# A three-block transformer layer on one core: layer-norm rows rebuilt from the transposed result, small reloads on the load queue, and one raw weight tile more in two rings

## The chip, the core and the metric

The kernel runs on one core of a Trainium2 chip. A core has five engines that work at the same time: TensorE (matmuls, called PE in the profile; PEld are its weight loads), VectorE (DVE), ScalarE (ACT), GpSimd (POOL) and SyncE (SP), which here only issues DMAs. Each engine takes its instructions in order, and semaphores hold an instruction until what it needs is there. Data live in device memory, in the on-chip memory SBUF (128 partitions) and in PSUM, where matmuls write: eight banks of 128 x 512 float32. POOL cannot read PSUM.

The metric is the device time in microseconds (us) of one execution. The kernel before took 5420.15 us, the median of three runs from 5416.47 to 5428.44 us.

## The reference

One layer over 512 tokens of width 2048, in float32. Three sub-layers follow one another, each added to its input and normalised:

```python
h = hybrid_mixer(x, ...)             # mLSTM heads + 16 forgetting-attention heads, gated, merged
x = layer_norm(DN_ALPHA * x + h, ln_w[0], ln_b[0])
h = memory_cross_attention(x, mem, w_xq, w_xkv, w_xo)     # 256 memory rows
x = layer_norm(DN_ALPHA * x + h, ln_w[1], ln_b[1])
h = peer_ffn(x, peer_wq, peer_sub_keys, peer_u, peer_v)   # 16 of 16384 experts per head and token
x = layer_norm(DN_ALPHA * x + h, ln_w[2], ln_b[2])
```

`layer_norm` takes mean and variance over the 2048 features of a token, and scales and shifts each feature: `(x - mu) * rsqrt(var + eps) * w + b`.

## The kernel before

**Tokens and stages.** The 512 tokens are four blocks of 128. Block 0 (`A` in the code) is computed first through the whole mixer, since the others need its state; blocks 1 to 3 (`B`, 384 tokens) follow. On the time axis of the profile: the first stage (to 870 us) is block 0's mixer, and between its groups `memory` projects the 256 memory rows; then (to 1620) `tail_a` takes block 0 through its output projection, both norms, the cross attention and the choice of its experts, alternating with the mLSTM heads of B; then B's `branch_ml` and `fox` (to 2550), `merge`, `residual`, `norm`, `cross`, `residual`, `norm` (to 3290), and B's `query` and top-k. From 3421 the experts: 288 tokens are computed densely over all 16384 experts (`stage_a`, `stage_h`, `stage_o`), and the experts of block 0 and of the last 96 tokens are gathered row by row by indirect DMAs on POOL with multiply-adds on DVE (`gathered`), a side job that `load_w` and `fill` advance a step at a time.

**A weight tile's way.** Every matmul operand is split into a high part (fp32r) and the remainder, and a product is three matmuls. A weight tile of 128 x 1024 comes by a DMA on SP's queue into a tile `raw`; ACT casts it to `whi` (L120); DVE (L123) or, for every `SHARE`-th tile, POOL (L122) subtracts to `wlo`. `raw` is free for the next load once `wlo` is written, so the number of raw tiles (4 in ring `w1` of the first stage, 5 in `w2`, 3 in `w3`, 2 in the ring `V` of the experts' second matrix) says how many loads are under way. `group_ws` holds the weights stationary and uses four large PSUM banks, `group_as` one bank for each token block. There are five large banks (tag `mm`) and three for small work (`sm_bank`).

**A norm.** `residual` leaves rows `r[t][g]` (128 tokens x 512 features; `t` the block, `g` the quarter) and their statistics. `norm` (L595) centres and scales the rows, turns each 128 x 128 piece with a TensorE transpose into a small bank, applies the weight and bias there, where they are one number for each partition, and splits the result into the operand pair of the next product (`X1`, `X2`). Then, for the rows that the next residual adds, it loads weight and bias broadcast over the partitions (L620, L621), multiplies and adds them on POOL (L624, L625; one block on DVE in B's second norm) and stores the rows to scratch memory (L626, `x1d` or `x2d`).

**Order.** The program is written as generators, and a scheduler orders each engine's instructions before the run, so that neighbours in the program can change places within what data and tiles allow; on the chip the order is fixed. Pools reuse memory of earlier pools: a new tile waits for the last use of what lay there. When B's second norm is done, the rows, the attention's tiles and operands are given up, and the tiles of the top-k and of ring `V` take their place.

**Other lines named below.** L956 and L995 reload the mLSTM output `htd` and the attention output `ytd` of B from scratch memory, by DMAs on POOL's queue, into three tiles `hr` and six tiles `t`. L454 is the sigmoid that empties the banks of a gate group of `branch_ml`, L737 the copy of a query group, L751 block 0's expert numbers, L797 and L784 the row updates of the gathered experts, L1028 the load of the 16 sub-key matrices, on ACT's queue. L318 and L327 empty the memory projections' banks into a tile `mo` that POOL's queue stores.

Of the kernel before, what the change touches and what calls it, by code (L numbers as in the profile page):

```python
# [10 lines left out]
F32 = mybir.dt.float32  # L11
# [5 lines left out]
ALU = mybir.AluOpType  # L17
# [14 lines left out]
NDENSE = 288  # L32
GATHERED = ((64, 64), (32, 32))
GB = 48
SHARE = 4
NEG = -1.0e30
ALPHA = 2.0 ** 0.25
EPS = 1e-5
# [8 lines left out]
def build(tc, I, out):  # L47
    nc = tc.nc
    with ExitStack() as ctx:
# [5 lines left out]
        def weights(stack, name, raw, hi, lo):  # L55

            W.update(pool=stack.enter_context(tc.tile_pool(name=name, bufs=1, reuse_waits="tile")), raw=raw, hi=hi, lo=lo)

        xs, x0 = ctx.enter_context(ExitStack()), ctx.enter_context(ExitStack())
        xbp = xs.enter_context(tc.tile_pool(name="x_b", bufs=1))  # L60
        weights(x0, "w1", 4, 3, 2)
        xap = x0.enter_context(tc.tile_pool(name="x_a", bufs=1))

        cnt, turn = [0], [0]
# [240 lines left out]
        def memory(mp):  # L305

            MT = []
            for kt in range(8):
                raw = load_raw(I["memT"][kt], 512)
                a, b = pair(mp, "mt", [P, 512], 16)  # L310
                split(a, b, raw)
                for kk in range(2):
                    MT.append((a[:, kk * MEM:(kk + 1) * MEM], b[:, kk * MEM:(kk + 1) * MEM]))
            for g in range(4):
                def ev_mk(s, b, g=g, k=[]):
                    if s % 2 == 0:
                        k.append(mp.tile([P, 512], F32, tag="mo", bufs=2, name=nm("mo")))
                    nc.scalar.copy(k[-1][:, (s % 2) * MEM:(s % 2 + 1) * MEM], b[:, :MEM])  # L318
                    if s % 2:
                        nc.gpsimd.dma_start(kmd[g, s // 2], k[-1])  # L320

                group_ws(I["w_xkv"][g], MT, MEM, ev_mk)
                yield
            for g in range(4):
                def ev_mv(t, b, g=g):
                    v = mp.tile([P, 512], F32, tag="mo", bufs=2, name=nm("mo"))
                    nc.vector.tensor_copy(v, b)  # L327
                    nc.gpsimd.dma_start(vmd[g, t], v)

                group_as(I["w_xkv"][4 + g], MT, 2, ev_mv)  # L330
                yield
# [260 lines left out]
            nc.vector.scalar_tensor_tensor(sts[:, :, 27], sts[:, :, 24], -1.0, sts[:, :, 26],  # L592
                                           op0=ALU.mult, op1=ALU.mult)

        def norm(R, r, sts, i, dst, cpair, tmp, o, vec=()):  # L595

            for c in range(NK):
                if c % 4 == 0:
                    for t in range(R.nb):
                        y = r[t][c // 4]  # L600
                        if (t + c // 4) % 2:
                            nc.scalar.activation(y, y, AF.Identity, scale=sts[:, t, 26:27], bias=sts[:, t, 27:28])
                        else:
                            nc.vector.tensor_scalar(y, y, sts[:, t, 24:25], sts[:, t, 26:27],
                                                    op0=ALU.subtract, op1=ALU.mult)
                bank = sm_bank()
                for t in range(R.nb):
                    nc.tensor.transpose(bank[:, t * P:(t + 1) * P], r[t][c // 4][:, (c % 4) * P:(c % 4 + 1) * P], ident)
                o.append(cpair())
                w, bb = lnwT[:, i, c:c + 1], lnbT[:, i, c:c + 1]  # L610
                f = tmp(R.n)
                if c % 2:
                    nc.scalar.activation(f, bank[:, :R.n], AF.Identity, scale=w, bias=bb)
                else:
                    nc.vector.tensor_scalar(f, bank[:, :R.n], w, bb, op0=ALU.mult, op1=ALU.add)
                split(*o[-1], f)
            work["hold"] = False
            for g in range(4):
                w, bb = tmp(512), tmp(512)
                nc.gpsimd.dma_start(w, I["ln_w"][i, g * 512:(g + 1) * 512].partition_broadcast(P))  # L620
                nc.gpsimd.dma_start(bb, I["ln_b"][i, g * 512:(g + 1) * 512].partition_broadcast(P))  # L621
                for t in range(R.nb):
                    e = nc.vector if t in vec else nc.gpsimd
                    e.tensor_mul(r[t][g], r[t][g], w)  # L624
                    e.tensor_add(r[t][g], r[t][g], bb)  # L625
                    nc.gpsimd.dma_start(dst[R.b0 + t, :, g], r[t][g])  # L626


        def cross(R, pool, X1, qt, kvt, pt, opair, O):
# [232 lines left out]
        work["share"] = SHARE  # L862
        with tc.tile_pool(name="sa", bufs=1, side="right", reuse_waits="tile") as sa:
            def aq(n=P):
                return sa.tile([P, P], F32, tag="q", bufs=12, name=nm("aq"))

            def at(n=512):
                if n == P:
# [113 lines left out]
        with tc.tile_pool(name="xb", bufs=1, reuse_waits="tile") as xp:  # L982
# [25 lines left out]
            norm(B, r, sts[1], 1, x2d, cpair, tmp, X2, vec=(1,))  # L1008
        x3.close()
        while work["jobs"] is not None:  # L1010
            if next(work["jobs"], None) is None:
# [12 lines left out]
               for t in range(1, TB)}  # L1024

        with tc.tile_pool(name="topk", bufs=1, reuse_waits="tile") as tp:
            keysT = tp.tile([P, 16, P], F32, tag="keysT", name="keysT")
            nc.scalar.dma_start(keysT, I["keysT"])  # L1028
            scs, QB = {}, []
            for g, _ in enumerate(query(B, X2, lambda: tp.tile([P, B.n], F32, tag="qT", bufs=6, name=nm("qT")), QB)):  # L1030
                for t in range(TB - 1, 0, -1):
                    bank = sm_bank()
                    for j in range(4):
                        nc.tensor.matmul(bank[:, j * P:(j + 1) * P], QB[g][j][:, (t - 1) * P:t * P],
                                         keysT[:, 4 * g + j, :], start=True, stop=True)
                    first = t == TB - 1
                    scs[t, g] = tp.tile([P, 512], F32, tag=f"sc{first}", bufs=2 if first else 8, name=nm("sc"))
                    nc.scalar.copy(scs[t, g], bank)
# [244 lines left out]
```

## Time and profile before

| | |
|---|---|
| median of three runs | 5420.15 us (5416.47 to 5428.44) |
| profiled execution | 5381.62 us, span 5379.9 us |
| mean granted TensorE clock | 0.965 |
| busy: PE, DVE, ACT, POOL | 4856.5, 3778.6, 2109.8, 1691.1 us |
| DMA | 1429 MB, mean 266 GB/s |

All durations come from the one profiled execution, whose own time is 38.5 us below the median of the three runs. A matmul's end in the profile is modelled, and matmuls overlap: the step from one start to the next tells more than the duration. A row of a group of instructions reads: line, engine, operation, output <- inputs, shapes, count | busy time, mean of one in ns | idle time of the engine just before them, and what ended it. A row of waits reads: who waited <- for whom: total us, times, longest us; SPq is the load queue of SP.

### The profile page before, as it was taken

To read this page: it belongs to the slowest core of one execution; us is meant where nothing else is said; L and a number is where in the kernel's file an instruction comes from. 1 tells how busy PE (TensorE), PEld (TensorE's weight loads), DVE (VectorE), ACT (ScalarE), POOL (GpSimd) and SP (SyncE) were. 2 spreads that over 40 slices of the span, in tenths; PEclk is the share of its full clock that TensorE was granted. 3 is DMA by queue.
4 is the path that set the end of the run, shared out by engine and by line. 5 is a ranking of instruction groups with operands and counts; after the bars stand their busy time and mean duration, and the time that the engine had idled before them with its cause. 6 is when DMAs were issued, how large, how long until landed. Compare 5 with 4: busy or idle time off the path is not lost. (4 is left out here: it accounts for less than half of the span.)

```text
span 5379.9 us, 74574 instructions
## 1 busy us (share of the span) xinstructions
PE 4856.5 (90%) x28273; PEld 4387.9 (82%) x28273; DVE 3778.6 (70%) x5275; ACT 2109.8 (39%) x3016; POOL 1691.1 (31%) x1279
## 2 busy tenths in 40 slices
PE   7988889999988999998997986999899999998886
PEld 5766667878867999887977865999899999997776
DVE  7655556654596777666867667797667778776777
ACT  6555555444442233332323332334343343333222
POOL 2333343322245544333545325220011112122221
PEclk8999999999998999999999998999999999999998
DMA  7777777555558988776976766466688888888885
GB/s 241 251 271 265 255 262 250 184 195 177 189 205 313 351 330 311 280 267 241 356 272 233 276 234 242 168 219 215 200 301 323 338 303 350 308 328 296 319 317 192
DMA packets 405193, 1429.38 MB, mean 266 GB/s; under 512 B 93468, under 2 KB 125852, under 8 KB 345664
## 3 DMA queue, kind: packets, MB, share of 16 engines
q1 hardware_dynamic: 242848, 819.80, 42.8%
q0 software_dynamic: 94016, 565.74, 28.1%
q10 hardware_dynamic: 67968, 39.07, 2.5%
q8 instruction: 221, 3.62, 0.3%
q14 instruction: 140, 1.15, 0.1%
HBM read 1351.71 MB, written 72.62 MB: 265 GB/s over the span
## 5 line engine op out<-in xcount | busy, mean ns | idle before, releaser
L120 ACT CAST whi<-raw 128x1024 fp32r<-128x1024 f32 x1472 | 1536.2, 1051 | 2373.0 <-PE mm L163 990.2
L123 DVE TENSOR_TENSOR wlo<-raw,whi 128x1024 fp32r<-128x1024 f32 x1232 | 1603.5, 1311 | 893.5 <-ACT whi L120 516.0
L122 POOL TENSOR_TENSOR wlo<-raw,whi 128x1024 fp32r<-128x1024 f32 x240 | 609.8, 2541 | 962.4 <-ACT whi L120 524.2
L797 DVE SCALAR_TENSOR_TENSOR xacc<-rows,dots,xacc 128x2048 f32<-128x2048 f32 x224 | 571.6, 2552 | 164.5 <-DMA rows<-in_peer_v,eid 163.8
L770 POOL DMA_INDIRECT rows<-in_peer_u,eid x224 | 319.3, 1425 | 1094.1 <-DVE wlo L123 303.0
L784 DVE SCALAR_TENSOR_TENSOR rows<-rows,xacc 128x2048 f32<-128x2048 f32 x224 | 530.7, 2374 | 157.7 <-DMA rows<-in_peer_u,eid 154.9
L163 PE MATMUL po<-hph,whi 128*128 128x288 f32 x2048 | 570.1, 304 | 55.6 <-ACT whi L120 39.9
L770 POOL DMA_INDIRECT rows<-in_peer_v,eid x224 | 329.1, 1469 | 915.5 <-DVE hpl L123 397.9
L163 PE MATMUL pa<-Ch,whi 128*128 128x288 f32 x2048 | 567.2, 301 | 41.0 <-ACT whi L120 39.6
L163 PE MATMUL pa<-Cl,whi 128*128 128x288 f32 x2048 | 563.8, 299 | 0.0
L163 PE MATMUL po<-hpl,whi 128*128 128x288 f32 x2048 | 563.2, 301 | 0.0
L163 PE MATMUL mm<-whi,xh 128*128 128x512 f32 x1088 | 438.2, 403 | 28.6 <-ACT whi L120 27.9
L163 PEld LDWEIGHTS po<-hph,whi 128*128 128x128 f32 x2048 | 394.1, 194 | 69.7 <-ACT whi L120 49.1
L163 PE MATMUL mm<-xh,whi 128*128 128x384 f32 x1280 | 432.3, 340 | 1.8 <-ACT c L551 1.4
L163 PE MATMUL mm<-xl,whi 128*128 128x384 f32 x1280 | 432.1, 339 | 0.0
L163 PEld LDWEIGHTS pa<-Ch,whi 128*128 128x128 f32 x2048 | 392.5, 192 | 45.7 <-ACT whi L120 42.1
L163 PE MATMUL mm<-whi,xl 128*128 128x512 f32 x1088 | 429.3, 395 | 0.0
L163 PEld LDWEIGHTS po<-hpl,whi 128*128 128x128 f32 x2048 | 395.0, 194 | 0.0
L163 PEld LDWEIGHTS pa<-Cl,whi 128*128 128x128 f32 x2048 | 392.3, 192 | 0.8 <-issue 0.8
L163 PE MATMUL mm<-wlo,xh 128*128 128x512 f32 x1088 | 327.4, 410 | 47.7 <-POOL wlo L122 26.1
L163 PE MATMUL po<-hph,wlo 128*128 128x288 f32 x2048 | 336.5, 300 | 34.8 <-DVE wlo L123 34.7
L163 PE MATMUL pa<-Ch,wlo 128*128 128x288 f32 x2048 | 327.4, 297 | 6.3 <-DVE wlo L123 6.3
(435 smaller groups left out, 8615.9 us busy)
## 6 DMA issues: line engine op xcount, KB each, us to landing
raw<-in_w_in SPq DMA_DIRECT2D x512, 512.0 KB, 4.6
raw<-in_vq SPq DMA_DIRECT2D x256, 512.0 KB, 5.6
raw<-in_uT SPq DMA_DIRECT2D x256, 512.0 KB, 4.5
raw<-in_w_xkv SPq DMA_DIRECT2D x64, 512.0 KB, 4.6
raw<-in_w_br_ml SPq DMA_DIRECT2D x64, 512.0 KB, 4.6
raw<-in_w_br_fx SPq DMA_DIRECT2D x64, 512.0 KB, 5.4
raw<-in_w_out SPq DMA_DIRECT2D x64, 512.0 KB, 4.2
raw<-in_w_xq SPq DMA_DIRECT2D x64, 512.0 KB, 3.3
```

Of the source, the lines that this page charges most:

```text
L120: nc.scalar.copy(hi, src)
L122: return nc.gpsimd.tensor_sub(lo, src, hi.bitcast(F32))
L123: return nc.vector.tensor_sub(lo, src, hi.bitcast(F32))
L163: nc.tensor.matmul(o, w if stat else x, x if stat else w, start=k == first and x is xh and not part, stop=k == last and part == 1)
L770: i = nc.gpsimd.indirect_dma_start(out=rows, out_offset=None, in_=I[table], in_offset=bass.IndirectOffsetOnAxis(ap=ei[:, k:k + 1], axis=0))
L784: nc.vector.scalar_tensor_tensor(rows, rows, 1.0, xacc, op0=ALU.mult, op1=ALU.mult, accum_out=dots[:, k:k + 1])
L797: nc.vector.scalar_tensor_tensor(xacc, rows, dots[:, k:k + 1], xacc, op0=ALU.mult, op1=ALU.add)
```

## The change

Five things change at once.

1. `norm` turns the scaled result back: for each quarter `g` it takes one large bank for each block; each scaled and shifted piece `f` is transposed once more into it, ACT copies the bank over the row tile, and that is stored. The broadcast loads, the multiplication and the addition of rows are gone, and so is the parameter `vec`.
2. `SHARE` goes from 4 to 8: POOL makes every eighth low part in place of every fourth, DVE the others, in all stages up to the top-k.
3. The reloads of `htd` and `ytd` are issued by SP. The sub-keys come in four loads of 256 KB by SP, two tiles, in place of one of 1 MB by ACT.
4. Ring `w1` has five raw tiles in place of four, ring `V` three in place of two.
5. To make room, `mo` has one tile in place of two, and the tag `q` of block 0's 128 x 128 tiles ten in place of twelve.

```diff
-SHARE = 4
+SHARE = 8
...
-        weights(x0, "w1", 4, 3, 2)
+        weights(x0, "w1", 5, 3, 2)
...
-                        k.append(mp.tile([P, 512], F32, tag="mo", bufs=2, name=nm("mo")))
+                        k.append(mp.tile([P, 512], F32, tag="mo", bufs=1, name=nm("mo")))
...
-                    v = mp.tile([P, 512], F32, tag="mo", bufs=2, name=nm("mo"))
+                    v = mp.tile([P, 512], F32, tag="mo", bufs=1, name=nm("mo"))
...
-        def norm(R, r, sts, i, dst, cpair, tmp, o, vec=()):
-
-            for c in range(NK):
-                if c % 4 == 0:
+        def norm(R, r, sts, i, dst, cpair, tmp, o):
+
+            for g in range(4):
+                for t in range(R.nb):
+                    y = r[t][g]
+                    if (t + g) % 2:
+                        nc.scalar.activation(y, y, AF.Identity, scale=sts[:, t, 26:27], bias=sts[:, t, 27:28])
+                    else:
+                        nc.vector.tensor_scalar(y, y, sts[:, t, 24:25], sts[:, t, 26:27],
+                                                op0=ALU.subtract, op1=ALU.mult)
+                back = [mm_bank() for _ in range(R.nb)]
+                for s in range(4):
+                    c, sl = 4 * g + s, slice(s * P, (s + 1) * P)
+                    bank = sm_bank()
                     for t in range(R.nb):
...
+                        nc.tensor.transpose(bank[:, t * P:(t + 1) * P], r[t][g][:, sl], ident)
+                    o.append(cpair())
+                    w, bb = lnwT[:, i, c:c + 1], lnbT[:, i, c:c + 1]
+                    f = tmp(R.n)
+                    if s % 2:
+                        nc.scalar.activation(f, bank[:, :R.n], AF.Identity, scale=w, bias=bb)
+                    else:
+                        nc.vector.tensor_scalar(f, bank[:, :R.n], w, bb, op0=ALU.mult, op1=ALU.add)
+                    split(*o[-1], f)
+                    for t in range(R.nb):
+                        nc.tensor.transpose(back[t][:, sl], f[:, t * P:(t + 1) * P], ident)
                 for t in range(R.nb):
...
+                    nc.scalar.copy(r[t][g], back[t])
+                    nc.gpsimd.dma_start(dst[R.b0 + t, :, g], r[t][g])
             work["hold"] = False
-            for g in range(4):
-                w, bb = tmp(512), tmp(512)
-                nc.gpsimd.dma_start(w, I["ln_w"][i, g * 512:(g + 1) * 512].partition_broadcast(P))
-                nc.gpsimd.dma_start(bb, I["ln_b"][i, g * 512:(g + 1) * 512].partition_broadcast(P))
-                for t in range(R.nb):
-                    e = nc.vector if t in vec else nc.gpsimd
-                    e.tensor_mul(r[t][g], r[t][g], w)
-                    e.tensor_add(r[t][g], r[t][g], bb)
-                    nc.gpsimd.dma_start(dst[R.b0 + t, :, g], r[t][g])
...
-                return sa.tile([P, P], F32, tag="q", bufs=12, name=nm("aq"))
+                return sa.tile([P, P], F32, tag="q", bufs=10, name=nm("aq"))
...
-                nc.gpsimd.dma_start(t, htd[j, :, B.cols])
+                nc.sync.dma_start(t, htd[j, :, B.cols])
...
-                nc.gpsimd.dma_start(y, ytd[j])
+                nc.sync.dma_start(y, ytd[j])
...
-            keysT = tp.tile([P, 16, P], F32, tag="keysT", name="keysT")
-            nc.scalar.dma_start(keysT, I["keysT"])
             scs, QB = {}, []
             for g, _ in enumerate(query(B, X2, lambda: tp.tile([P, B.n], F32, tag="qT", bufs=6, name=nm("qT")), QB)):
+                keysT = tp.tile([P, 4, P], F32, tag="keysT", bufs=2, name=nm("keysT"))
+                nc.sync.dma_start(keysT, I["keysT"][:, 4 * g:4 * g + 4])
...
-        V = dict(pool=gap, raw=2, hi=3, lo=3)
+        V = dict(pool=gap, raw=3, hi=3, lo=3)
```

More of the change, by code (lines that the diff above doesn't have):

```diff
@@ L593, in residual @@
                                            op0=ALU.mult, op1=ALU.mult)
-        def norm(R, r, sts, i, dst, cpair, tmp, o, vec=()):
-            for c in range(NK):
-                if c % 4 == 0:
-                    for t in range(R.nb):
[L600 to L606, printed above, removed]
-                for t in range(R.nb):
[L608 to L616, printed above, removed]
-            work["hold"] = False
-            for g in range(4):
-                w, bb = tmp(512), tmp(512)
-                nc.gpsimd.dma_start(w, I["ln_w"][i, g * 512:(g + 1) * 512].partition_broadcast(P))
-                nc.gpsimd.dma_start(bb, I["ln_b"][i, g * 512:(g + 1) * 512].partition_broadcast(P))
-                for t in range(R.nb):
-                    e = nc.vector if t in vec else nc.gpsimd
-                    e.tensor_mul(r[t][g], r[t][g], w)
-                    e.tensor_add(r[t][g], r[t][g], bb)
-                    nc.gpsimd.dma_start(dst[R.b0 + t, :, g], r[t][g])
@@ L1007, in build @@
                          tmp, r, sts))
-            norm(B, r, sts[1], 1, x2d, cpair, tmp, X2, vec=(1,))
+            norm(B, r, sts[1], 1, x2d, cpair, tmp, X2)
         x3.close()
@@ L1034, in build @@
                         nc.tensor.matmul(bank[:, j * P:(j + 1) * P], QB[g][j][:, (t - 1) * P:t * P],
-                                         keysT[:, 4 * g + j, :], start=True, stop=True)
+                                         keysT[:, j, :], start=True, stop=True)
                     first = t == TB - 1
```

## The prediction

> **What bounds the kernel now.** I read the table of engines first, then busy time in stretches cut at the kernel's stages, then who waited for whom inside the stretches that showed idle TensorE time.
>
> ```profile
> PE 4856.5 (90%) x28273; PEld 4387.9 (82%) x28273; DVE 3778.6 (70%) x5275; ACT 2109.8 (39%) x3016; POOL 1691.1 (31%) x1279
> ```
>
> ```profile
> 0.00:870.00 870.00, 741.40 (x3425) 555.70 (x3426) 530.83 (x745) 510.14 (x672) 309.73 (x251) 0.97 0.76 258
> 870.00:1620.00 750.00, 702.57 (x3344) 587.40 (x3342) 476.24 (x847) 343.18 (x472) 237.25 (x170) 0.99 0.55 193
> 1620.00:2550.00 930.00, 876.42 (x4736) 822.03 (x4736) 653.23 (x746) 290.58 (x417) 409.70 (x289) 0.97 0.82 301
> 2840.00:3060.00 220.00, 199.33 (x1042) 183.37 (x1043) 160.19 (x137) 75.58 (x126) 109.17 (x92) 0.96 0.67 245
> 3060.00:3290.00 230.00, 172.57 (x788) 144.34 (x786) 163.82 (x134) 59.06 (x74) 106.11 (x85) 0.89 0.70 257
> 3965.00:4920.00 955.00, 938.38 (x7020) 930.66 (x7019) 716.99 (x780) 363.75 (x462) 168.18 (x123) 1.00 0.85 321
> 4920.00:5350.00 430.00, 349.51 (x2284) 326.14 (x2284) 326.93 (x386) 117.52 (x140) 79.43 (x62) 0.93 0.78 294
> ```
>
> Columns: stretch, length, busy time of PE, PEld, DVE, ACT, POOL, granted clock, DMA share, GB/s. TensorE carries the span, but unevenly. Length minus PE gives its idle time: 128.6 us in the first stage (block 0 and the memory projections), 47.4 us from 870 to 1620, 20.7 and 57.4 us around the two norms of blocks 1 to 3, only 16.6 us in the long part of the experts' loop and 80.5 us in its last 430 us. The change touches both ends and the norms, not the tight middle.
>
> In the first stage the weights come late:
>
> ```profile
> PE mm L163 <- ACT whi L120: 42.8, 62, 2.4
> PE mm L163 <- POOL wlo L122: 37.8, 37, 6.2
> PE mm L163 <- DVE wlo L123: 23.1, 34, 2.7
> ```
>
> ```profile
> SPq L128 <- DVE wlo L123: 318.2, 211, 7.2
> SPq L128 <- POOL wlo L122: 215.6, 73, 4.1
> ```
>
> 103.7 of the 128.6 us end on the high or low part of a weight tile, and the queue that issues the loads stands 533.8 us waiting for a low part to release a raw tile. The stage is held by the number of raw tiles, not by the bytes: DMA share is 0.76, and 0.85 elsewhere.
>
> **The change part by part.**
>
> *Five raw tiles for four, and every eighth low part on POOL instead of every fourth.*
>
> ```profile
> L120 ACT CAST whi<-raw x385: 1029/1049/1086, 21.4 to 868.2; 128x1024 fp32r<-128x1024 f32 x193
> ```
>
> ```profile
> 601.31 0.39 PE L163 MATMUL mm<-whi,xl 128*128 128x512 f32 x1
> 601.53 0.39 PE L163 MATMUL mm<-whi,xh 128*128 128x512 f32 x1
> ```
>
> 385 tiles in 846.8 us are 2.20 us each, so a raw tile's turn (load, high part, low part) is 4 x 2.20 = 8.8 us. The same turn over five tiles gives 1.76 us: 385 x 0.44 = 169 us. The other end is nothing, if landing times grow by what the fifth tile adds. Matmuls start 0.225 us apart, six for each of block 0's 321 tiles (1.35 us) and at most twelve such (2.7 us) for the 64 of the memory projections: 606 us of 870, so TensorE permits the whole gain; DVE, at 531 us plus 48 low parts of 1.31 us (row below), reaches 594. I take 75 us, near the middle and within the 104 us that idle rows confirm; range 0 to 169.
>
> ```profile
> L123 DVE TENSOR_TENSOR wlo<-raw,whi 128x1024 fp32r<-128x1024 f32 x1232 | 1603.5, 1311 | 893.5 <-ACT whi L120 516.0 <-PE mm L163 351.1 <-issue 10.5
> ```
>
> ```profile
> L122 POOL TENSOR_TENSOR wlo<-raw,whi 128x1024 fp32r<-128x1024 f32 x240 | 609.8, 2541 | 962.4 <-ACT whi L120 524.2 <-PE mm L163 340.4 <-DVE st L205 23.4
> ```
>
> Half of 240 low parts move: POOL loses 120 x 2.541 = 305 us, DVE gains 120 x 1.311 = 157 us, 72 of them (94 us) after the first stage. There TensorE is the bound and DVE is at 60 to 75%, so I cost them at nothing; that cover is gone if DVE's queue runs late (rival D).
>
> *The memory projections' output tile, two to one.*
>
> ```profile
> L320 POOL DMA_DIRECT2D kmd<-mo x8: 539/552/565, 154.1 to 454.3; - x8
> ```
>
> ```profile
> DMA to landing us min/median/max: 2.3/2.8/4.9
> ```
>
> Each of the 8 groups has its second eviction wait for the first tile's store: 0.6 us of issue plus 2.8 us to landing, on ACT or DVE, with weight casts queued behind. The built order puts two to four casts between, so I take 8 us of the possible 27. Ten 128x128 tiles for twelve: nothing; the most it can cost is the wait for a store like these.
>
> *The norm.* It drops 32 broadcast loads, their multiply and add on POOL (and DVE for one block), and adds one turn-back per turn, 128 in all, and 32 ACT copies of 128x512 (0.59 us each, as the score copies):
>
> ```profile
> L1038 ACT COPY sc<-sm x12: 586/586/605, 3321.1 to 3420.8; 128x512 f32<-128x512 f32 x12
> ```
>
> Turn-backs go into the five large PSUM banks, which the matmul groups behind need. The built order shows the effect. For block 0 the 16 turns of a norm had some 108 weight matmuls among them; now 29 of its first 32 stand in one run. Its stretch before:
>
> ```profile
> L608 PE MATMUL sm<-ident,ra x16: 270/272/272, 1049.4 to 1070.0; 128*128 128x128 f32 x16
> ```
>
> It is 20.6 us. TensorE, 94% busy there, can lose from nothing to all of it per norm; ACT needs 16 casts, 8 scalings and 4 copies, about 12 us by the neighbouring rows. I take 12 each: a loss of 24 us (0 to 41).
>
> For blocks 1 to 3 the first norm goes from 62 weight matmuls among its turns to 24, the second from 98 to 18. A 384-column matmul follows the next by 0.17 us:
>
> ```profile
> 3340.87 0.34 PE L163 MATMUL mm<-Ch,whi 128*128 128x384 f32 x1
> 3341.04 0.34 PE L163 MATMUL mm<-Cl,whi 128*128 128x384 f32 x1
> ```
>
> So 38 x 0.17 + 12 x 0.59 = 14 us lost at the first, 80 x 0.17 + 7 = 21 us at the second. What is gained:
>
> ```profile
> 3250.48 9.56 DVE L625 TENSOR_TENSOR ra<-ra,t 128x512 f32<-128x512 f32 x2
> 3259.96 2.34 DVE L797 SCALAR_TENSOR_TENSOR xacc<-rows,dots,xacc 128x2048 f32<-128x2048 f32 x1
> 3262.22 0.68 DVE L624 TENSOR_TENSOR ra<-ra,t 128x512 f32<-128x512 f32 x1
> 3262.82 8.33 DVE L123 TENSOR_TENSOR wlo<-raw,whi 128x1024 fp32r<-128x1024 f32 x2
> ```
>
> ```profile
> 2910.09 1.21 DVE L123 TENSOR_TENSOR wlo<-raw,whi 128x1024 fp32r<-128x1024 f32 x1
> ```
>
> ```profile
> 3291.70 1.04 ACT L120 CAST whi<-raw 128x1024 fp32r<-128x1024 f32 x1 [36.04 <-DMA x2d<-ra]
> ```
>
> ```profile
> PE mm L163 <- DVE wlo L123: 59.6, 58, 10.8
> PE mm L163 <- POOL wlo L122: 51.7, 41, 7.1
> ```
>
> Two low parts that otherwise take 1.22 us each (row below) took 8.33 together while POOL multiplied rows: that is TensorE's 10.8 us wait. The next ACT cast stands 36 us for the last row store, behind POOL's chain; TensorE loses 36.8 us to it. Both go. What is late next: in the new order three casts of V's tiles precede the query's third weight, and V's tiles need the memory that the row stores free.
>
> ```profile
> raw<-in_vq SPq DMA_DIRECT2D x256, 512.0 KB, 5.6
> ```
>
> ```profile
> x2d<-ra POOLq DMA_DIRECT2D x12, 256.0 KB, 5.4
> ```
>
> Store 5.4 us, load 5.6, three casts 3.2, less about 4 us of matmuls in hand: 10 us. Second norm: 47.6 - 21 - 10 = 17 us gained (-20 to 45). First norm: the 7.1 us wait (it stands at 2888) and some 3 of smaller ones gone against 14, so 4 us lost.
>
> The Trainium skill's page "SBUF — State Buffer", section "Who interferes with whom", says that a DVE instruction with two SBUF inputs and a GpSimd one that reads SBUF shut each other out for a whole instruction. The rows agree: 9.56 us for two additions that take 0.68 each alone.
>
> *Reloads of h and of y on SP instead of POOL.*
>
> ```profile
>   PE mm L163: 42.4, 8
> ```
>
> ```profile
> 1619.84 1.28 ACT L454 ACT_TABLE_LOAD   x1 [6.79 <-DVE eid L751]
> 1621.13 1.26 ACT L454 ACTIVATE sg<-mm 128x384 f32<-128x384 f32 x3
> ```
>
> The first is TensorE's wait for h's parts, in the view of the tile it is reloaded into. 27 of the 42 us stay: ACT holds the sigmoid that frees the banks until block 0's top-k ends on DVE at 1619, and that is not moved. Of the other 15 I take 12 (0 to 25): SP has issued its weights by about 1601, 17 us ahead of POOL. On SP each reload waits for one of three tiles, with later weight loads behind it; the order puts six reloads ahead of the first, whose group is not due yet. y: 2 us. Key tiles: nothing.
>
> The skill's "DMA: Bandwidth & Descriptors", section "Issuing engines are not separate DMA queues", has all issuers share the 16 engines, so that another queue saves only issue time; by that the 12 would be near 0 and the sum 12 us worse. No row before shows these loads on SP.
>
> *Three raw tiles for V.*
>
> ```profile
> ACT whi L120 <- DMA raw<-in_vq: 229.1, 77, 10.7
> ```
>
> ```profile
> L120 ACT CAST whi<-raw 128x1024 fp32r<-128x1024 f32 x92 | 96.5, 1049 | 276.9 <-DMA raw<-in_vq 229.1 <-PE po L163 25.2 <-DVE wlo L123 12.6
> ```
>
> ```profile
> 4521.48 12.72 PE po L163 x94
> ```
>
> In the last 430 us nothing but V is loaded as weights: 92 tiles, 4.67 us each, a turn of 9.3 us on two. A third makes 3.1 us, under TensorE's 24 x 0.135 = 3.25. The ends: nothing, and what the next limit allows: DVE's 327 us, or DMA, whose 430 x 0.78 = 335 us at the 0.85 reached before it is 395 us, so 35 us, or 74 us at a share of 0.94. I take 50, and 5 of the 16.6 us ahead of it.
>
> **The sum**: 75 - 8 - 24 - 4 + 17 + 12 + 2 + 50 + 5 = 125 us off. The profiled execution took 5381.6 us (span 5379.9 and 1.7 around), the median shown is 5420.2, 38.5 us more, which I carry: 5382 - 125 = 5257, or 5295 against the median.
>
> **Rivals.**
>
> *A, both rings gain in full.* The load queue waits for raw tiles most of the first stage, and TensorE and DVE have room; against it, that needs a fifth more than the stage's 258 GB/s. First stage 140, last part 74: 5295 - 65 - 24 = 5206.
>
> *B, the fifth tile waits in the DMA queues.* Landing then grows with requests, and the first stage gains 5 us: 5365. For it, DMA is already at 0.76; against it, 0.85 at 321 GB/s later on.
>
> *C, the norm holds TensorE.* All 41 us of block 0's norms, and the second later norm loses 20 instead of gaining 17: 5295 + 17 + 37 = 5349.
>
> *D, DVE becomes the feeder (slower).* Place: all stages before the experts' loop. Price: the 157 us of low parts, if TensorE waits for every one; 5295 + 157 = 5452. It decides once more than 125 us (80%) reaches TensorE. For it, DVE works in order and holds 2.3 us row updates; against it, DVE's low parts now cost TensorE 59.6 us of waits in these groups over the whole run, and DVE's mean of 1311 ns stands over some 1.22 us undisturbed, 110 us in 1232, of which fewer POOL instructions should give back a part.
>
> By the skill's lock rule above, each POOL low part also stops DVE, so halving them returns DVE time, and D would stay under its 125 us. The trace agrees as far as it shows: the two low parts above took 8.33 us while POOL worked.
>
> **Chances and range.** Forecast 0.57, with 5235 to 5355 as its own range; A 0.11, B 0.12, C 0.09, D 0.11. About 0.2% (11 us) is what a measurement here can tell from no change. B and C together would bring it there: I put 0.05 of them on "same". Faster 0.57 + 0.11 + 0.16 = 0.84 (given as 0.83), slower 0.12 with D. The range runs from 5195, half of A outside, to 5425, D outside.
>
> **What would show it.** First stage shorter by 40 to 110 us with a DMA share above 0.8 and less waiting of the load queue; no 36 us ACT wait before the query; TensorE idle 10 us or more in each of block 0's norms; waits for V under 100 us at the end. The forecast is wrong if V's or w_in's landing time grows by over a third, or if TensorE's waits for DVE's low parts pass 120 us.

## The result, and the profile after

The changed kernel took 5215.26 us, the median of four runs (5202.03 to 5231.18), against 5424.3 us for the kernel before beside it (5416.47 to 5430.11): a ratio of 0.9617, 95% interval 0.9586 to 0.9648, some 209 us less. The forecast was 5295 us, 125 us less. The profiled execution took 5231.18 us (span 5229.4), 16 us above its median, while the one of before had been 38.5 us below its own; so the two traces differ by only 150 us. A second trace of the kernel before was therefore taken (below), and stands in the table. Lengths run from the first or last matmul of a named group to the next, in us; a gain is counted from the second trace (the whole span: 182 us).

| stretch | before | before, second | after | gain |
|---|---|---|---|---|
| first stage, to the last memory product | 871.8 | 876.8 | 790.2 | 86.6 |
| from there to B's first gate product (block 0's norms) | 751.4 | 751.4 | 769.1 | -17.7 |
| B's mLSTM gate groups | 258.4 | 258.7 | 258.4 | 0.3 |
| from there to the last turn of B's `fox` | 663.2 | 668.9 | 683.4 | -14.5 |
| from there to B's second norm | 661.5 | 664.5 | 652.0 | 12.5 |
| second norm and `query`, to the experts' first product | 214.7 | 217.1 | 183.3 | 33.8 |
| from there to the first output product | 543.8 | 543.7 | 550.3 | -6.6 |
| the loop with ring `V`, to the last output product | 1379.0 | 1394.2 | 1302.3 | 91.9 |
| from there to the end | 36.1 | 36.3 | 40.4 | -4.1 |

The first row of the page after, and its two kinds of low part:

```profile
PE 4823.5 (92%) x28401; PEld 4393.5 (84%) x28401; DVE 3730.6 (71%) x5387; ACT 2119.6 (41%) x3047; POOL 1289.7 (25%) x1039
...
L123 DVE TENSOR_TENSOR wlo<-raw,whi 128x1024 fp32r<-128x1024 f32 x1352 | 1680.0, 1256 | 809.2 <-ACT whi L120 389.6
...
L122 POOL TENSOR_TENSOR wlo<-raw,whi 128x1024 fp32r<-128x1024 f32 x120 | 304.9, 2541 | 938.2 <-ACT whi L120 447.5
```

POOL lost 401 us of work, with the norm's rows and half of its low parts; DVE made 120 low parts more and is still not busier, and each takes 1256 ns in the mean in place of 1311. The stretches after, cut at the same events (columns as in the prediction: stretch, length, busy PE, PEld, DVE, ACT, POOL, granted clock, DMA share, GB/s):

```profile
0.00:790.00 790.00, 715.80 (x3432) 558.67 (x3433) 555.54 (x794) 509.04 (x674) 197.54 (x201) 0.98 0.83 284
790.00:1510.00 720.00, 690.74 (x3240) 572.39 (x3238) 409.91 (x720) 337.56 (x468) 108.35 (x97) 0.98 0.56 188
...
1819.00:2504.00 685.00, 634.98 (x3394) 582.94 (x3392) 463.94 (x591) 216.52 (x328) 218.04 (x180) 0.97 0.77 279
...
3134.00:3333.00 199.00, 162.59 (x938) 159.14 (x939) 153.16 (x283) 71.57 (x105) 66.04 (x48) 0.90 0.70 252
...
3887.00:4893.00 1006.00, 1001.37 (x7528) 997.01 (x7527) 793.47 (x879) 388.38 (x494) 207.69 (x137) 1.00 0.90 337
4893.00:5190.00 297.00, 254.77 (x1767) 241.62 (x1767) 242.71 (x278) 89.63 (x108) 65.11 (x47) 0.96 0.83 315
```

Length minus PE: the first stage idles 74 us in place of 129, the experts' loop 4.6 + 42.2 = 47 us in place of 97. The first stage's waits after, TensorE's and then the load queue's (who waited <- for whom: total, times, longest):

```profile
PE mm L163 <- ACT whi L120: 23.2, 27, 9.6
PE mm L163 <- DVE wlo L123: 22.0, 29, 2.3
...
PE mm L163 <- POOL wlo L122: 2.6, 4, 1.3
```

```profile
SPq L128 <- DVE wlo L123: 340.2, 241, 4.3
SPq L128 <- POOL wlo L122: 117.8, 38, 7.4
```

TensorE's waits from B's second norm to the end of the query, the longest one before and then the two longest after:

```profile
PE mm L163 <- ACT qT L737: 36.8, 1, 36.8
```

```profile
PE sm L610 <- DVE ra L603: 19.6, 1, 19.6
PE mm L163 <- ACT whi L120: 9.4, 1, 9.4
```

ACT's waits for V in the last stretch after:

```profile
ACT whi L120 <- DMA raw<-in_vq: 117.2, 49, 10.5
```

The 36.8 us wait for the query's copy is gone, and the 9.4 us wait that takes its place is the forecast one, for the query's third weight. The 19.6 us are the wait for the first centred row, 18.9 us before.

### The profile page after: what moved, and what is told of

It reads as the page before. It is cut to its first block, busy times and chain, and to the rows that moved or that the text cites. A ratio compares the mean times of both kernels' runs of the same rounds, so it can differ in the third digit from the quotient of the medians.

```text
span 5229.4 us, 74718 instructions
## 1 busy us (share of the span) xinstructions
PE 4823.5 (92%) x28401; PEld 4393.5 (84%) x28401; DVE 3730.6 (71%) x5387; ACT 2119.6 (41%) x3047; POOL 1289.7 (25%) x1039
## 5 line engine op out<-in xcount | busy, mean ns | idle before, releaser
L123 DVE TENSOR_TENSOR wlo<-raw,whi 128x1024 fp32r<-128x1024 f32 x1352 | 1680.0, 1256 | 809.2 <-ACT whi L120 389.6
L795 DVE SCALAR_TENSOR_TENSOR xacc<-rows,dots,xacc 128x2048 f32<-128x2048 f32 x224 | 536.1, 2393 | 177.8 <-DMA rows<-in_peer_v,eid 176.6
L163 PE MATMUL pa<-Ch,whi 128*128 128x288 f32 x2048 | 566.0, 300 | 47.6 <-ACT whi L120 46.1
L163 PE MATMUL po<-hph,whi 128*128 128x288 f32 x2048 | 553.1, 299 | 24.9 <-DVE acc L1169 13.9
L768 POOL DMA_INDIRECT rows<-in_peer_v,eid x224 | 340.8, 1522 | 931.0 <-DVE xacc L795 314.2
L163 PE MATMUL po<-hpl,whi 128*128 128x288 f32 x2048 | 551.0, 297 | 0.0
L122 POOL TENSOR_TENSOR wlo<-raw,whi 128x1024 fp32r<-128x1024 f32 x120 | 304.9, 2541 | 938.2 <-ACT whi L120 447.5
L163 PE MATMUL mm<-whi,xh 128*128 128x512 f32 x1088 | 435.3, 400 | 12.9 <-ACT whi L120 10.1
L163 PE MATMUL po<-hph,wlo 128*128 128x288 f32 x2048 | 332.3, 297 | 14.3 <-DVE wlo L123 14.3
```

The lines of the kernel that those rows point to most:

```text
L122: return nc.gpsimd.tensor_sub(lo, src, hi.bitcast(F32))
L123: return nc.vector.tensor_sub(lo, src, hi.bitcast(F32))
L163: nc.tensor.matmul(o, w if stat else x, x if stat else w, start=k == first and x is xh and not part, stop=k == last and part == 1)
L768: i = nc.gpsimd.indirect_dma_start(out=rows, out_offset=None, in_=I[table], in_offset=bass.IndirectOffsetOnAxis(ap=ei[:, k:k + 1], axis=0))
L795: nc.vector.scalar_tensor_tensor(xacc, rows, dots[:, k:k + 1], xacc, op0=ALU.mult, op1=ALU.add)
```

## The experiments

Twelve kernels ran, one of them the kernel before once more. Each ratio is to runs of the kernel before beside it; a difference of two ratios is turned into time with 5424 us and is uncertain by some 20 us, so smaller effects are read from the traces. These are sharper: seven traces of kernels with the same first stage end it between 787.6 and 791.6 us.

### The tile rings

`w1_four`, the changed kernel with

```diff
-        weights(x0, "w1", 5, 3, 2)
+        weights(x0, "w1", 4, 3, 2)
```

> The changed kernel with four raw tiles in the first stage's ring in place of five; everything else as changed. My step (the first stage is held by the number of raw tiles; the SHARE edit is worth nothing): the first stage ends near 865 us instead of 790, and the median is about 75 us above the changed kernel's 5215, so 5290. Rival (POOL's slow low parts held the raw tiles, and the SHARE edit made the gain): the first stage still ends at 790 to 805 and the median is 5215 to 5230. Between them, about 830 and 5255, both edits carry it.

Measured: 5285.35 us (5271.15 to 5289.46), ratio 0.9755 (0.9726 to 0.9783); by ratio 75 us above the changed kernel, 70 by the medians. The first stage ended at 851.3 us, 61 us later.

```profile
0.00:853.00 853.00, 749.07 (x3437) 550.47 (x3438) 556.03 (x796) 512.36 (x674) 196.62 (x202) 0.98 0.80 263
```

The row is 63 us longer than the changed kernel's of 790 us, but only 104 - 74 = 30 us of that are idle time. The other 33 are counted as TensorE's busy time, for the same products and at the same granted clock of 0.98. A 128x512 product is shown as 0.39 us long where the next can start after 0.225, so a short wait between two hides in it; of some 2300 steps between the starts of such products, 963 are longer than 0.235 us here, and 740 in the changed kernel.

`before_w1_five`, the kernel before with

```diff
-        weights(x0, "w1", 4, 3, 2)
+        weights(x0, "w1", 5, 3, 2)
...
-                    v = mp.tile([P, 512], F32, tag="mo", bufs=2, name=nm("mo"))
+                    v = mp.tile([P, 512], F32, tag="mo", bufs=1, name=nm("mo"))
...
-                return sa.tile([P, P], F32, tag="q", bufs=12, name=nm("aq"))
+                return sa.tile([P, P], F32, tag="q", bufs=10, name=nm("aq"))
```

> The kernel before with the fifth raw tile in the first stage's ring, and the two smaller tags that make room for it, as the only edits. My step: 75 - 8 = 67 us faster, 5354. By the stages seen so far (five tiles and SHARE 4 ended the first stage at 810, against 872 to 877): 62 to 67 us faster, 5354 to 5360. Rival (the tile's effect depends on SHARE 8): less than 50 us.

Measured: 5342.46 us (5330.27 to 5359.4), ratio 0.9837 (0.9820 to 0.9853), 88 us faster. Its first stage ends at 816.5 us, 55 to 60 us earlier than in the two traces of before. So the fifth tile is worth 55 to 61 us of the first stage, with either `SHARE`, and 70 to 88 us of the time. The third tile of the other ring, `v_two`, is the changed kernel with

```diff
-        V = dict(pool=gap, raw=3, hi=3, lo=3)
+        V = dict(pool=gap, raw=2, hi=3, lo=3)
```

> The changed kernel with two raw tiles in the ring of the experts' second matrix in place of three. My step: 55 us slower (50 in the last stretch, 5 ahead of it), median 5270; the two traces (from the gate build to the end of the last output product) say 77, median 5292. Rival (the third tile only waits in the DMA queues, and the gain came from elsewhere, as from gathered rows that were done earlier): less than 20 us slower, median under 5235.

Measured: 5325.81 us (5309.78 to 5332.42), ratio 0.9826 (0.9796 to 0.9856): 110 us slower, twice my term. Its experts' loop and ACT's waits for V in the last stretch:

```profile
3879.00:4846.00 967.00, 941.50 (x7008) 932.97 (x7007) 712.30 (x772) 363.74 (x461) 162.57 (x119) 0.99 0.86 314
4846.00:5290.00 444.00, 352.55 (x2294) 330.07 (x2293) 328.10 (x384) 118.72 (x142) 82.00 (x65) 0.92 0.79 292
```

```profile
ACT whi L120 <- DMA raw<-in_vq: 246.2, 83, 11.2
```

The loop is 1411 us long, against 1303 after. Of the 108 us, TensorE's idle time makes 117 - 47 = 70, and its busy time 1294 - 1256 = 38 for the same products: the granted clock is 0.92 in the last stretch, against 0.96. Matmul steps at a slow clock, which the last section shows, cost 40 us in this loop and 13 after, so 27 of the 38; the rest was not taken apart.

`before_again` is the kernel before, unchanged.

> The kernel before once more, unchanged, for a second profiled execution. The shown one took 5381.6 us, 25 to 50 us less than every timed run of it. If that execution was a lucky one where the ring of two raw tiles for the experts' second matrix is fed (the two-tile version of the changed kernel spends 1956 us from the first product of the experts to the last output product, the shown trace of before 1923), this trace has some 1950 to 1960 there, a span of 5405 to 5425, and its first stages end within 5 us of 872, 1623 and 2545. If instead the profiler makes every execution of this kernel quicker, the span is near 5380 again and that stretch near 1923.

Measured: 5429.29 us (5413.31 to 5437.88), ratio 1.0 (0.999 to 1.0009), span 5411.6 us.

```profile
3981.00:4938.00 957.00, 938.10 (x7004) 931.05 (x7004) 711.80 (x774) 363.01 (x460) 168.10 (x119) 0.99 0.86 317
4938.00:5376.00 438.00, 351.42 (x2297) 329.45 (x2296) 327.94 (x382) 118.30 (x142) 74.52 (x65) 0.92 0.80 296
```

The shown execution was a quick one. From the experts' first product to the last output product, five traces with two tiles in ring `V` take 1923, 1938, 1937, 1940 and 1957 us, the shown one least; eight traces with three tiles take 1846 to 1854. With the third tile this stretch also scatters less, by 8 us in place of 34; the timed runs of a whole kernel do not (29 us over the four of the changed kernel, 25 over the ten of this one).

### The norm

`old_norm` is the changed kernel with the earlier `norm`, and `vec=(1,)` in its last call:

```diff
-        def norm(R, r, sts, i, dst, cpair, tmp, o):
+        def norm(R, r, sts, i, dst, cpair, tmp, o, vec=()):
...
+            for g in range(4):
+                w, bb = tmp(512), tmp(512)
...
-            norm(B, r, sts[1], 1, x2d, cpair, tmp, X2)
+            norm(B, r, sts[1], 1, x2d, cpair, tmp, X2, vec=(1,))
```

> The changed kernel with the earlier norm (broadcast loads of weight and bias, rows multiplied and added on POOL, one block on DVE). My steps: block 0's two norms lose 24 us as changed, so the stretch from 790 to the last top-k product shortens from 720 to about 697; B's first norm 4 us better; the way from the second residual to the end of the query 17 us longer (199 to 216 us, 31 by the two traces). Together the median stays within 10 us of 5215. Rival (the norm brings more than it costs everywhere): the block-0 stretch stays at 720 and the median rises by 20 to 35 us, to 5235 to 5250.

Measured: 5212.98 us (5200.88 to 5220.9), ratio 0.9619 (0.9593 to 0.9645): no difference in sum. But the parts are large. From block 0's first norm to B's first gate product it takes 564.6 us, against 594.5 with the new norm: 30 us are lost there. (Counted from the end of the first stage it is 25, 744.1 against 769.1, since the new norm makes its first turn 5 us sooner.) From B's second norm to the experts 212.8 against 183.3: 30 us are won, and the long wait is there again:

```profile
PE mm L163 <- ACT qT L737: 42.7, 1, 42.7
```

At B's first norm (to the start of the second) it is 362 against 361. The greater part of block 0's loss is seen in the matmuls around block 0's second norm, first with the earlier norm, then with the new one (count, shortest/median/longest ns, first and last start; `xh` is B's mLSTM work, `Ch` the query of block 0):

```profile
L163 PE MATMUL mm<-whi,Ch x64: 389/397/501, 1404.4 to 1465.8; 128*128 128x512 f32 x64
...
L163 PE MATMUL mm<-whi,xh x41: 387/390/487, 1374.8 to 1402.5; 128*128 128x512 f32 x41
```

```profile
L163 PE MATMUL mm<-whi,xh x48: 387/389/482, 1398.0 to 1429.6; 128*128 128x512 f32 x48
```

```profile
L163 PE MATMUL mm<-whi,Ch x64: 391/397/798, 1437.3 to 1496.7; 128*128 128x512 f32 x64
```

The norm's first turn is at 1385.7 and 1391.6 us. The earlier one has the mLSTM group among its turns, and the query starts at 1404; the new one's turns stand together (the last turn-back at 1407.5), the group follows, and the query starts at 1437. What comes after for block 0 is later too, and it sets the start of B's gate products; from the second norm's first turn to the following rows of ACT it is 144.6 us with the earlier norm and 164.4 with the new one:

```profile
1530.31 1.28 ACT L454 ACT_TABLE_LOAD   x1 [6.12 <-DVE selA_i L714]
```

```profile
1555.97 1.28 ACT L454 ACT_TABLE_LOAD   x1 [6.12 <-DVE selA_i L712]
```

Both are the sigmoid that stands behind block 0's top-k in ACT's order; TensorE's idle gap ahead of it is 31.2 and 26.8 us. The stretch from the second norm to the first gate products, with the earlier norm and with the new one:

```profile
1386.00:1550.00 164.00, 127.33 (x616) 107.94 (x615) 139.84 (x357) 75.11 (x120) 58.71 (x47) 0.89 0.62 213
```

```profile
1392.00:1575.00 183.00, 147.28 (x699) 122.75 (x698) 137.93 (x361) 80.76 (x128) 45.11 (x37) 0.90 0.58 198
```

TensorE idles 36 to 37 us in both, and in the longer one it does 83 matmuls more. So the new norm's price behind its second use, 20 of the 30 us, is not idle time but work that was moved into the chain of block 0. The other 10 us are lost from the first norm's first turn to the second's. There TensorE's idle time grows from 4.6 to 12.9 us, and 5.9 of these are a wait for the second norm's centred rows (it is 4.1 ahead of the first norm).

`norm_mixed` takes the earlier norm for block 0 and the new one, renamed, for B:

```diff
-            norm(B, r, sts[0], 0, x1d, cpair, tmp, X1)
+            norm_b(B, r, sts[0], 0, x1d, cpair, tmp, X1)
...
-            norm(B, r, sts[1], 1, x2d, cpair, tmp, X2)
+            norm_b(B, r, sts[1], 1, x2d, cpair, tmp, X2)
```

> The changed kernel with the earlier norm for block 0 alone, and the new one for blocks 1 to 3. If the two effects are independent: the front part of the run with the earlier norm (fox ends near 2470 instead of 2504, 30 us better) and the back part of the changed kernel (835 us from there to the first product of the experts, against 867 with the earlier norm), so a median of 5180 to 5190, 30 us under 5215. If what is lost in block 0 is made up elsewhere anyway (the same gathered rows have to be done in any case), 5205 to 5220.

Measured: 5186.37 us (5175.24 to 5200.86), ratio 0.9544 (0.9528 to 0.9560), 29 us under the changed kernel by the medians and 40 by the ratios. B's gate products start at 1532.2 us, and the way from the end of `fox` to the experts takes 834.7, as with the new norm (835.3). So the two effects are independent, as far as these traces tell.

### The share of low parts on POOL

`share_four`, the changed kernel with

```diff
-SHARE = 8
+SHARE = 4
```

> The changed kernel with every fourth low part on POOL again in place of every eighth. My step (SHARE costs and brings nothing): first stage ends at 790 to 800, the stretch of the forgetting attention (from the last mLSTM head group at 1819 to 2504) stays at 685 us, median 5215 to 5225. Rival (SHARE made the first stage's gain): first stage ends near 850, median 5275. Second question: if the 19 us that this stretch lost come from low parts moved to DVE, it goes back to 666 here; if not, it stays near 685.

Measured: 5219.31 us (5218.37 to 5228.66), ratio 0.9644 (0.9619 to 0.9669): little difference in sum, again of two larger ones. Its first stage ends at 809.6, 19 us later, with TensorE's waits for POOL back:

```profile
PE mm L163 <- POOL wlo L122: 18.6, 30, 2.2
```

And its stretch to the end of `fox` is shorter, 661.6 in place of 683.4:

```profile
1834.00:2497.00 663.00, 630.01 (x3393) 580.17 (x3393) 462.85 (x575) 219.28 (x330) 268.88 (x196) 0.98 0.79 289
```

`before_share8`, the kernel before with

```diff
-SHARE = 4
+SHARE = 8
```

> The kernel before with SHARE 8 as the only edit. My step: no change, median 5420. By the stages seen so far: the first stage 21 to 25 us shorter (four raw tiles and SHARE 8 ended at 851, four and SHARE 4 at 872 and 877), the stretch of the forgetting attention 20 us longer (685 against 663 to 669), so again 5410 to 5425, by two effects that cancel. Rival (DVE becomes the feeder): slower by 20 us and more, 5440 or above.

Measured: 5397.11 us (5390.22 to 5404.44), ratio 0.9948 (0.9932 to 0.9965), 28 us faster: in the kernel before, the edit is worth something by itself. The first stage ended at 858.1, 14 to 19 us earlier, and the attention's stretch took 673.1, only 4 to 10 us longer.

`mixed_share` is norm_mixed with

```diff
+            work["share"] = 4
             run(fox(B, fp, lambda n: fp.tile([P, n], F32, tag="c", bufs=16, name=nm("c")), hold_r))
```

> As norm_mixed, and from blocks 1 to 3's forgetting attention on every fourth low part on POOL again (every eighth before). If the 20 us that this stretch lost come from low parts that DVE makes ahead of the attention's small steps: the stretch takes 662 to 666 us instead of 685, and the median is 5160 to 5170. If not, or if the gathered rows' work only moves: within 5 us of norm_mixed.

The edit holds from `fox` on, up to the top-k. Measured: 5171.11 us (5167.01 to 5173.77), ratio 0.9522 (0.9506 to 0.9538), 15 us under norm_mixed by the medians and 12 by the ratios. `fox`'s stretch takes 658.7 us; norm_mixed's and its own:

```profile
1790.00:2476.00 686.00, 636.98 (x3392) 584.53 (x3391) 466.66 (x591) 216.77 (x328) 208.03 (x180) 0.96 0.77 279
```

```profile
1792.00:2452.00 660.00, 631.66 (x3392) 581.63 (x3391) 464.37 (x575) 219.41 (x330) 272.17 (x196) 0.98 0.80 290
```

TensorE idles 49 us in the one and 28 in the other. Over all traces this stretch takes 658.7 to 668.9 us in seven traces of kernels that make every fourth low part there on POOL, and 673.1 to 685.2 in the seven others. Sixteen more of DVE's low parts there cost time; which of the attention's small steps they delay was not tried apart.

`share_sixteen` is mixed_share with

```diff
-SHARE = 8
+SHARE = 16
```

> As mixed_share (5171), with every sixteenth low part on POOL, in place of every eighth, up to blocks 1 to 3's forgetting attention (from there every fourth, as in mixed_share). From four to eight the first stage gained 16 us (first norm of block 0 at 981 and 965). If POOL's slow low parts are what was saved, half of it again: 8 us, first stage ends near 781, median 5163. If DVE has become the feeder: first stage unchanged or longer, median 5171 or more.

Measured: 5155.42 us (5155.27 to 5156.72), ratio 0.9500 (0.9484 to 0.9515), 16 us under mixed_share by the medians and 12 by the ratios; with `v_four` below it is the fastest kernel here. The first stage ends at 773.0, another 16 us earlier, at a DMA share of 0.85:

```profile
0.00:773.00 773.00, 708.72 (x3432) 556.61 (x3432) 550.70 (x818) 504.68 (x672) 137.01 (x179) 0.99 0.85 290
```

### The reloads, and a fourth tile for V

`reload_pool`, the changed kernel with

```diff
-                nc.sync.dma_start(t, htd[j, :, B.cols])
+                nc.gpsimd.dma_start(t, htd[j, :, B.cols])
...
-                nc.sync.dma_start(y, ytd[j])
+                nc.gpsimd.dma_start(y, ytd[j])
```

> The changed kernel with the reloads of the mLSTM output and the attention output on POOL's queue again. My step: 14 us slower (0 to 27), median 5229, the gap ahead of the first gate product of blocks 1 to 3 growing from 27 to about 40 us. Rival (block 0's top-k holds ACT and with it the banks; the reload's queue does not matter): the gap stays at 27 and the median at 5210 to 5220.

Measured: 5216.05 us (5210.02 to 5222.05), ratio 0.9601 (0.9585 to 0.9617): no loss. The gap ahead of the first gate product is the same 26.8 us (first row after, then this kernel), and the wait is ACT's, whose sigmoid stands behind block 0's top-k in both:

```profile
PE mm L163 <- ACT Hh L120: 27.7, 2, 26.8
```

```profile
PE mm L163 <- ACT Hh L120: 28.9, 2, 26.8
```

`v_four` is mixed_share with five tiles `qT` in place of six, and

```diff
-        V = dict(pool=gap, raw=3, hi=3, lo=3)
+        V = dict(pool=gap, raw=4, hi=3, lo=3)
...
-                keysT = tp.tile([P, 4, P], F32, tag="keysT", bufs=2, name=nm("keysT"))
+                keysT = tp.tile([P, 4, P], F32, tag="keysT", bufs=1, name=nm("keysT"))
```

> As mixed_share (5171), with four raw tiles in the ring of the experts' second matrix in place of three; to make room one key tile in place of two and five tiles for the query rows in place of six. If the loads still hold that loop after the third tile (68 waits of ACT for them, 167 us, in the changed kernel's loop): 10 to 20 us less, median 5150 to 5160. If DMA is at its limit there (share 0.90 and 337 GB/s) or TensorE and DVE are: within 5 us of 5171. If the smaller query tiles hold up the top-k: the stretch ahead of the experts grows by more than 5 us.

Measured: 5156.76 us (5144.34 to 5159.23), ratio 0.9504 (0.9488 to 0.9520), 14 us less by the medians and 10 by the ratios, whose intervals overlap. The trace is clearer: the loop from the first output product on takes 1285.7 us, against 1300 to 1307 in the eight traces with three tiles. The stretch ahead of it, 542.1, is no sign of the tile, for it takes 543 to 551 in those eight. The query did not become longer (167.7 us from B's second norm's end to the experts, against 166.1). The two changes of v_four and share_sixteen were not tried together.

## Why the prediction was right or wrong

The sign was right and the time lay in the range from 5195 to 5425, but below 5235 to 5355, the range that I gave the forecast itself; the gain was 209 us where 125 were forecast. By its own steps:

*The fifth raw tile and `mo`: right.* Forecast 75 - 8 = 67; measured 55 to 61 us of the first stage and 70 to 88 of the time. Two of the copies into `mo`'s one tile waited for a store, 2.8 us together, not 8. Rival B falls: the median landing of a raw tile grew from 4.5 us to between 4.9 and 5.2 (six traces with the same first stage), about a tenth, while the stage gained.

*Three raw tiles for V: mechanism right, size half.* Forecast 55, measured 110. Against the shown trace, the idle time that went is 97 - 47 = 50 us, which is the term. Two things were not in it: the shown execution idled 97 us where the two later ones with two tiles idle 105 and 117, and TensorE's busy time for the same products was 32 to 38 us longer, 21 to 27 of it in slow steps. The landing time of V's tiles grew from between 5.6 and 5.8 us to between 6.9 and 7.6 (the other traces with three tiles), by a fifth to just over a third, the sign that I had named for a wrong forecast; but the DMA share rose too, and the tiles came more often. Waits for V in the last stretch are 117 us, not under 100.

*Block 0's norms: right in sum, wrong in how.* Forecast 24 lost (0 to 41), measured 25 from the end of the first stage and 30 from the first turn. I priced it as lost overlap in each norm; of the 30, 10 are lost from the first norm to the second and 20 behind the second, where the displaced group holds up the chain to block 0's top-k. The sign that I named, 10 us of idle time in each norm, did not appear (it was 4.1 and 5.9), so it is in part luck that the size came near.

*B's norms: under-valued.* Forecast -4 and +17, measured +1 and +30. The 9.4 us wait for the third weight came as forecast. The failed step is the 21 us for lost overlap at the second norm. The stretch before, cut like the one quoted of after:

```profile
3187.00:3417.00 230.00, 156.37 (x890) 152.03 (x888) 171.56 (x288) 66.16 (x92) 101.42 (x76) 0.84 0.63 226
```

TensorE's idle time fell from 73.6 us to 36.4, which is the 47.6 - 10 us that I had counted, and its busy time rose by 6 us alone, in place of 21. Rival C falls with it.

*The reloads on SP: wrong.* Forecast 14, measured nothing. I took the 15 us of waits outside the gap for queueing on POOL; on SP the same waits remain (43.0 us in all at the reloaded tiles, against 42.4 before and 37.5 with the reloads put back). The failed step is that term. The reading by the Trainium skill's page "DMA: Bandwidth & Descriptors", section "Issuing engines are not separate DMA queues", that another queue saves only the time of issuing, so near 0 here, was the better one.

*`SHARE`: costed at nothing; wrong in its parts.* It won 14 to 25 us in the first stage, where POOL's 2.5 us low parts had held raw tiles and TensorE, and lost 4 to 26 in the attention. By itself it was worth 28 us in the kernel before, and little in the changed one. Rival D falls as a whole: TensorE's waits for DVE's low parts went from 59.6 + 34.7 + 6.3 = 100.6 to 40.2 + 14.3 + 5.5 = 60.0 us over the run. In one place, the attention, the low parts that moved to DVE did cost time.

*The median.* I carried 38.5 us from the profiled execution to the median. It was no constant of the kernel: the second trace took 31.7 us more than the shown one, 15 of them in the loop with ring `V` and 5 to 6 each in the first stage and in `fox`'s stretch, and the profiled execution after lies 16 us above its own median. This is why the timed gain (209) is above that of the shown traces (150).

Taken out one at a time, the parts give 75 + 113 + 15 + 1 - 9 = 195 of the 208 us by ratio; the rest is within their errors, so no further cause is needed. What the smaller tags cost and the sub-keys' loads bring was not tried apart. Rival A, both rings in full, came nearest to the time (5206), but not by its mechanism alone: the first stage gained 82 to 87 us, not 140.

## What to carry to other kernels

Price a load ring by more than the consumer's idle time: with one tile too few, short waits hide in its busy time (33 us in the first stage here), longer ones bring steps at a slow clock behind them (27 us in the experts' loop), and one profiled execution may be a lucky one. When a step is made denser, ask which work it displaces and onto whose chain that work falls, not how long the step itself idles. An edit that is neutral in sum can be two opposite effects in two stages: apply it in the stage where it wins (here 5171 us, and 5155 with a larger `SHARE` in the first stages, against 5215 for the change as a whole).

## What the runs showed that I had not expected

A wait of TensorE can cost more than its length. The kernel before, its last stretch, in order of time (start, us, operation, count, idle time before it):

```profile
4915.28 0.69 PE L163 MATMUL po<-hph,whi 128*128 128x288 f32 x4
4925.17 0.61 PE L163 MATMUL po<-hph,whi 128*128 128x288 f32 x1 [9.20 <-ACT whi L120]
4925.58 0.44 PE L163 MATMUL po<-hpl,whi 128*128 128x288 f32 x1
4925.82 0.44 PE L163 MATMUL po<-hph,whi 128*128 128x288 f32 x1
...
4931.60 0.30 PE L163 MATMUL po<-hpl,whi 128*128 128x288 f32 x1
4931.73 0.29 PE L163 MATMUL po<-hph,whi 128*128 128x288 f32 x1
```

Behind the wait the starts are 0.24 us apart, six microseconds later 0.13. The granted clock of the same moments (columns as in the prediction) is 0.50, then 1.00:

```profile
4925.10:4931.30 6.20, 6.13 (x25) 6.13 (x26) 3.14 (x4) 1.06 (x2) 0.00 (x0) 0.50 1.02 415
4931.30:4936.00 4.70, 4.70 (x37) 4.70 (x37) 3.44 (x8) 1.92 (x3) 0.00 (x0) 1.00 0.99 379
```

A short wait does it too, in the changed kernel:

```profile
4991.17 0.56 PE L163 MATMUL po<-hph,whi 128*128 128x288 f32 x1 [1.74 <-DVE acc L1169]
...
4991.77 0.44 PE L163 MATMUL po<-hph,whi 128*128 128x288 f32 x1
4992.01 0.44 PE L163 MATMUL po<-hpl,whi 128*128 128x288 f32 x1
```

The following is counted in all fourteen traces, in the experts' loop from the first output product to the last. A wait is the time by which a step from one product to the next exceeds the usual 0.13 us. Those of over 0.5 us that stand alone (no other begins in the 8 us before or the 6 us behind) were followed by five or more steps of 0.2 to 0.3 us in 0 of 45 cases below 1.5 us, in 17 of 43 from 1.5 to 2.5 us, and in 37 of 45 above; the slow steps then cost 1.6 us more in the mean (1.1 to 2.6). In the last stretch, such steps add 30 us before and 11 after. The Trainium skill's page "TensorE: Matmul & The Clock Gate", section "HAM oscillation — how this bites in real kernels", says that TensorE's idle gaps should stay under about 3.4 us; here most waits of 2.5 to 3 us already bring the slow clock, 17 of 21.
